# A streamed two-layer hybrid encoder: TensorE's order handed to the scheduler, more room ahead of side matmuls, memory held until DMAs have read it

## The chip, the cores and the metric

One core of one Trainium2 chip runs the whole program. The metric is the time of one execution on the device in microseconds (us). The kernel before was run three times. One further execution was taken by the hardware profiler; its trace gives the durations of instructions, waits and the granted TensorE clock.

## The reference

`x` is 256 positions by 2048 channels. Each of two layers normalises it, projects it into the columns of four token mixers and of four merge gates, mixes, projects each branch back to 2048 channels, merges by gates, and adds an output projection to the residual stream. All is float32.

```python
def hybrid_layer(x, ...):
    h = rms_norm(x, norm_g)
    proj = h @ w_in                       # (256, 2048) @ (2048, 15104)
...
    ya = a_bg * depthwise_conv(a_cg * a_x, conv_a_w) * silu(a_z)      # A: short convolution
    yb = gqa_attention(rope(rms(q)), rope(rms(k)), v) * silu(b_z)     # B: grouped-query attention
    yc = rwkv7_bidir(h, c_r, c_k, c_v, ...) * silu(c_z)               # C: RWKV-7, both directions
    u = depthwise_conv(d_val * sigmoid(d_gate), dw_w) + dw_b          # D: 31 taps, LayerNorm, swish
    yd = silu(layer_norm(u)) * silu(d_z)
...
    g = sigmoid(gates.reshape(b, s, 4, 2048) + b_gate)
    merged = sum(g * (ys @ w_branch))
    return x + merged @ w_out
def reference(x, ...):
    for l in range(2):
        x = hybrid_layer(x, ...)
    return rms_norm(x, final_norm_g)
```

## The kernel before, in words

**The main stream.** The weights of both layers lie in memory as 612 chunks of 128 x 1024 floats (512 KB), in the order of `STREAM` (line 90): three tiles of the RWKV decay weights (`L`), the input projections of branches C, B, A and D, the merges of branches A and B taken in turn, the D gates, the merge of D, the C gates (`c_z`), the merge of C, and the output projection (`O`). Each chunk is loaded by SP into `raw` (4 buffers). ScalarE (ACT) rounds it to `hi` (3 buffers), VectorE (DVE) makes `lo = raw - hi` (2 buffers), and TensorE (PE) multiplies: `tile_b` (459) takes two chunks for one tile of 128 columns, each with eight 128x512 matmuls of `hi` and eight 128x256 matmuls of `lo`, into a PSUM buffer `mg` (3 buffers). The activations lie as rounded pairs in `slab` tiles (`operand`, 486). `tile_branch` (469) does the same for the branch outputs into `mb` (1 buffer). Then ACT and DVE move the PSUM buffer into the arena (`whole`, 477).

**The side work.** All that the branches do between projection and merge is written as Python generators: `branch_a`, `branch_b`, `branch_d`, `rwkv`, and under it `inverses`, which inverts blocks of 64, and `chunks`, which prepares a stretch of the scan. Their matmuls go into PSUM buffers `sd` (4 buffers). The scan of one RWKV direction (lines 945 to 1027) is a chain: a product of `bdE` and `bdT`, moved by ACT to `j3`; products of `j3`, moved to `ls` and `hs`; a product of those and of the state `s0`, moved by ACT to `bdS`; a transpose of `bdS` through PE; and its move by ACT to the next `s0`. Sums over a head go through `parts` (616), which makes `part` (1 buffer, a rounded copy by ACT and a remainder by DVE), and two matmuls against `rounded`. `branch_d` (740) has two LayerNorm sums over 512 channels, each a matmul `sd<-arena,consts` of `sq`.

**What sets the order.** The program is traced once in Python. Every engine call passes `Engine.call` (line 202 of the profile is its `return f(out, ...)`, so that nearly all instructions have that line), which keeps a model of time: `now` for PE, `clk` for DVE and ACT, `due` for when the last result of the step is ready, and `landed` for DMAs. After every main matmul `pump` (343) lets each generator go on whose time `at` has come. `step` (330) runs it to its next `yield c` and sets `at`: `now + c` for c above 0, and for `yield 0` the time at which its results are due plus `SLACK` = 0.4. `drain` (348) lets nothing but side work go on until a generator has ended; a merge does so with its branch. PE then keeps the traced order, since `run` (1338) puts both layers under `manual_schedule` for PE. The orders of the other engines are made by the tile framework's scheduler.

**Memory.** The working tiles lie in one tile, `arena`, that the kernel hands out itself (`Arena`, 103): `a` (255) takes words, `f` (282) gives them back with a time `when`, the latest of `now`, `due` and `clk`, plus `OVER` = 1.5. `get` prefers words whose time has passed. The framework orders any two instructions that touch the same words. `room` (274) makes a generator wait until enough words are free. In branch D, `sq` can thus come to lie in words that a DMA of `rwkv` still reads (the `COPY` of 64x1024 into `xt`, and the two DMAs `scratch<-arena` of `xi` and `xt`, behind the 31 steps of the inverse on DVE).

**The layers' boundary.** `project` (1277) makes the new `x` in eight pairs of tiles. At the last one (g = 7) of layer 0 it sums the squares with three matmuls `sd<-arena,consts`, the last two of which read the squares of the last two tiles, and `new_rstd` makes the factor `rbc`. The next layer's first 8 tiles (`RAW`) are multiplied by the unnormalised `x` and scaled by `rbc` in `evac` (560), while `normalise` (541) makes `h`.

Of the kernel before, what the change touches and what calls it, by code (L numbers as in the profile page):

```python
# [18 lines left out]
P = 128  # L19
D = 2048  # L20
S = 256
# [81 lines left out]
class Arena:  # L103
# [11 lines left out]
    def get(self, words, keep=False, take=True, now=0.0):  # L115


        m = -(-words // self.U)
        best = None
        i = 0  # L120
        while i < self.n:
            if self.used[i]:
                i += 1
                continue
            e = i
            while e < self.n and not self.used[e]:
                e += 1
            if e - i >= m:

                j = i if keep else e - m  # L130
                late = self.when[j:j + m].max() > now
                key = (late, j) if keep else (late, e - i - m, -i)
                if best is None or key < best[0]:
                    best = (key, j)
            i = e
        if best is None:
            if not take:
                return False
            raise MemoryError(f"arena: {words} words asked, {(~self.used).sum() * self.U} free, live "
                              + str(sorted((v[1] * self.U, v[2]) for v in self.live.values())))  # L140
        j = best[1]
        if not take:
            return True
        self.used[j:j + m] = True
        self.peak = max(self.peak, int(self.used.sum()) * self.U * 4)
        return j, m
# [66 lines left out]
class Kern:  # L213
# [5 lines left out]
    SLACK = 0.4  # L219
    OVER = 1.5  # L220
    LEAD = 1.7
    TWAIT = 24.0
# [51 lines left out]
    def room(self, words):  # L274

        e = self.cur
        e.want, e.net = 0, 0
        while self.arena.free() < words + 640 + sum(max(0, x.want - x.net) for x in self.side):
            yield 0.4
        e.want = words  # L280

    def f(self, *aps):
        for ap in aps:
            _, m, _, j = self.arena.live.pop(id(ap))
            self.arena.put(j, m, max(self.now, self.due, *self.clk.values()) + self.OVER)
            if self.cur:
                self.cur.purse.net -= m * Arena.U
# [17 lines left out]
    def pside(self):  # L305
        self.ring = self.ring[1:] + [self.now + 1.5]
        return self.psum("sd", 4)


# [20 lines left out]
    def step(self, e):  # L330
        self.due = max(self.now, e.due)
        self.landed = 0.0
        self.cur = e
        c = next(e.gen, None)
        self.cur = None
        e.due = max(self.due, self.landed)
        if c is None:
            e.alive = False
            self.side.remove(e)
        else:  # L340
            e.at = self.now + c if c > 0 else e.due + self.SLACK

# [72 lines left out]
    def fetch(self):  # L415
        nc = self.nc
        while len(self.raws) < 1 + self.FAR and self.load():
            pass
        if not self.raws:
            return False  # L420
        raw = self.raws.pop(0)
        hi = self.wtile("hi", 3, F32R)
        lo = self.wtile("lo", 2, F32R)
        with self.tc.high_priority():
            nc.scalar.activation(hi, raw, AF.Copy)
            nc.vector.tensor_tensor(lo, raw, hi.bitcast(F32), ALU.subtract)
        self.ready.append((hi, lo))
        return True

    def chunk(self):  # L430
        while len(self.ready) < self.AHEAD and self.fetch():
            pass
        return self.ready.pop(0)

# [66 lines left out]
    def first_x(self):  # L501
        nc = self.nc
        self.l = 0
        self.xT = [self.operand() for _ in range(4)]
        self.xs = [self.a([P, 4, S], True) for _ in range(4)]
        with self.tc.high_priority(), self.tc.manual_schedule(engines={SP, ACT, DVE}):
# [32 lines left out]
            self.f(sq)  # L539

    def normalise(self, h):

        nc = self.nc
        for x in self.xs:
            n = x.shape[1]
            for j in range(0, n, 2):
                t = self.a([P, 2, S])
                for i in range(2):
                    nc.vector.scalar_tensor_tensor(t[:, i], x[:, j + i], self.pc("norm_g", self.hk + i), self.rbc,
                                                   ALU.mult, ALU.mult)  # L550
                yield 0
                o = h[self.hk // 4][:, self.hk % 4:self.hk % 4 + 2]
                self.split(o[:, :, 0, :], o[:, :, 1, :], t)
                self.f(t)
                self.hk += 2
                yield 0.4
            self.f(x)


    def evac(self, out, ps):  # L560
        self.whole(out, ps)
        if self.raw:
            self.nc.vector.tensor_tensor(out, out, self.rbc, ALU.mult)
# [69 lines left out]
    def head_rstd(self, x):  # L633

        nc = self.nc
        out = self.a1()
        nc.scalar.activation(out, x, AF.Square)
        parts = self.parts(out)
        yield 0
        ps = self.pside()[:, :S]  # L640
        self.rsqrt(ps, 1.0 / 64, self.e_rms, out, self.exact(ps, self.bdr, parts))
        yield 0
        return out

    def norm_rope(self, x, rs, g, dst):
        nc = self.nc
        xn = self.a1()
        nc.vector.scalar_tensor_tensor(xn, x, g, rs, ALU.mult, ALU.mult)
        t = self.a1()
        nc.vector.tensor_tensor(t, xn, self.cos, ALU.mult)  # L650
        parts = self.parts(xn)
        yield 0
        ps = self.pside()
        self.exact(ps[:, :S], self.permr, parts)
        nc.vector.tensor_tensor(xn, ps[:, :S], self.sin, ALU.mult)
        for sl, d in dst:
            nc.vector.tensor_tensor(d, t[sl], xn[sl], ALU.add)
        self.f(t, xn)
        yield 0

    def branch_b(self, k, v, qz):
# [12 lines left out]
        for i in range(NT):  # L674
# [12 lines left out]
            for tb in range(2):  # L687
# [16 lines left out]
                pes.append(pe)  # L704
                yield 0
            self.f(qr)
            for tb, pe in enumerate(pes):
                ps = self.pside()
                for h in range(2):
                    for kb in range(2):  # L710
# [4 lines left out]
                                     ps.rearrange("p (h k t) -> p h k t", h=2, k=2), AF.Copy)  # L715
                yield 0
            ps = self.pside()
# [22 lines left out]
    def branch_d(self, acc, convs, dz):  # L740
# [11 lines left out]
        nc.vector.tensor_tensor(sq[:, 0], sq[:, 0], sq[:, 1], ALU.add)  # L752
        yield 0
        ps = self.pside()
# [5 lines left out]
        nc.vector.tensor_tensor(sq[:, 0], sq[:, 0], sq[:, 1], ALU.add)  # L760
        yield 0
        ps = self.pside()
# [24 lines left out]
    def rwkv(self, rkv, tl, cz):  # L787
# [5 lines left out]
        for d in range(2):  # L793
# [8 lines left out]
            for p0 in range(0, NT, 2):  # L802
# [42 lines left out]
                parts = self.parts(rs)  # L845
                yield 0
                ps = self.pside()
# [41 lines left out]
                parts = self.parts(r2)  # L889
                yield 0  # L890
                ps = self.pside()
# [9 lines left out]
                for p in (p0, p0 + 1):  # L901
                    bd = self.bd["K"][0]
                    nc.scalar.activation(bd[lo, :, 0:CH], v4(al[lo, p]), AF.Copy)
                    nc.scalar.activation(bd[hi, :, CH:], v4(al[hi, p]), AF.Copy)
                    yield 0
                    ps = self.pside()
# [47 lines left out]
            for p in range(NT):  # L954
# [71 lines left out]
                parts = self.parts(sq)  # L1026
                yield 0
                ps = self.pside()
# [32 lines left out]
    def inverses(self, bd, gs, scr, ready):  # L1061
# [22 lines left out]
        for h in range(2):  # L1084
            nc.scalar.activation(w1[h * 64:h * 64 + 32], ps[h * 64:h * 64 + 32], AF.Copy)
        yield 0
        ps = self.pside().rearrange("p (c n) -> p c n", c=n)
# [5 lines left out]
        for h in range(2):  # L1093
            nc.scalar.activation(t[h * 64 + 32:h * 64 + 64, :, h * 64:h * 64 + 32], ps[h * 64:h * 64 + 32], AF.Copy)
        ready.extend(range(NT))
        yield 0

    def chunks(self, n, out, bd, al, vv, kb, gs, rd):
# [14 lines left out]
        nc.scalar.activation(rb[hi, :, CH:], rd[hi, p, cs2], AF.Copy)  # L1113
        yield 0
        ps = self.pside()
# [24 lines left out]
        out.append((ex, mk, w))  # L1140
        yield 0

# [108 lines left out]
    def merge(self, l, br, g, acc, mT, gens):  # L1251

        nc = self.nc
        first, last = br == BR_ORDER[0], br == BR_ORDER[-1]
        z = self.a([P, 2, S], True)
        for j in range(2):
# [20 lines left out]
    def project(self, l, mT):  # L1277
# [8 lines left out]
        for g in range(8):  # L1286
# [4 lines left out]
            if g < 7:  # L1291
# [5 lines left out]
                if g == 0:  # L1297
                    sq = s
                else:
                    nc.vector.tensor_tensor(sq, sq, s, ALU.add)  # L1300
                    self.f(s)
            else:

# [21 lines left out]
            for j in range(2):  # L1325
                k = 2 * g + j
                self.split(xT[-1][:, k % 4, 0, :], xT[-1][:, k % 4, 1, :], xr[:, j], self.pc("norm_g", k))
        self.new_rstd(sums)
        self.f(sq)
        self.xT, self.xs = xT, xs  # L1330
        if not last:
            return
        for g in range(8):
            e = nc.gpsimd if g in (3, 6) else nc.vector
            e.tensor_tensor(xs[g], xs[g], self.rbc[:, None, :].to_broadcast([P, 2, S]), ALU.mult)
            (nc.sync if g % 2 else nc.scalar).dma_start(io["out"][:, 2 * g:2 * g + 2], xs[g])

    def run(self):
# [4 lines left out]
        self.first_x()  # L1343

        with self.tc.manual_schedule(engines={mybir.EngineType.PE}):
            for l in range(DEPTH):
                self.layer(l)

# [124 lines left out]
```

## Time and profile before

| | |
|---|---|
| median of three runs | 2014.15 us (2011.96 to 2016.07) |
| the profiled execution | 2011.95 us, of which its span is 2009.7 us |
| mean granted TensorE clock | 0.990 of full speed |
| busy share of the span | PE 96%, DVE 72%, ACT 63%, POOL 4% |
| weights read | 612 DMAs of 512 KB; 332.48 MB read in all, 170 GB/s over the span |

In the trace a row gives engine, operation, what is written and read, its shape, and in brackets how long the engine was idle before it and what released it. `sd`, `mg` and `mb` are PSUM buffers, `arena` is any working tile.

### The profile page before, as it was taken

The numbers are of one execution on the slowest core, as the hardware profiler recorded it, in microseconds if no ns is written. First come the engines' busy times: TensorE is split into PE (matmuls) and PEld (weight loads), VectorE is DVE, ScalarE is ACT, GpSimd is POOL, SyncE is SP. The second block draws the span as 40 slices with busy tenths as digits, with TensorE's granted clock in tenths as the row PEclk, the third lists the DMA queues.
The fourth block names the chain that finished last, engine by engine and source line by source line (L and its number), as shares of the span: only waits on it lengthen the run. The fifth ranks groups of instructions, "written<-read, shape, count | busy, mean of one in ns | idle before, by whom it ended". The sixth has DMA issues, their size and how long they took to land.

```text
span 2009.7 us, 32327 instructions
## 1 busy us (share of the span) xinstructions
PE 1934.0 (96%) x12194; PEld 1707.4 (85%) x12194; DVE 1447.7 (72%) x2495; ACT 1261.3 (63%) x2293; POOL 71.3 (4%) x117
## 2 busy tenths in 40 slices
PE   8999999999989999999999999999999899999997
PEld 6887888888978998898888878889888789988886
DVE  7767969977786656666677778699767765566665
ACT  6676677676547765554556766776764577655544
POOL 1001010000110000000000011000001100000000
PEclk9999999999999999999999999999999899999998
DMA  7545444455654445656655545344555544456653
GB/s 248 177 159 157 158 150 142 147 175 174 188 167 137 147 151 186 210 192 216 207 181 178 163 156 166 127 147 159 175 172 189 160 137 153 159 193 204 204 193 128
DMA packets 97692, 343.17 MB, mean 171 GB/s; under 512 B 11808, under 2 KB 12192, under 8 KB 97536
## 3 DMA queue, kind: packets, MB, share of 16 engines
q1 hardware_dynamic: 93312, 331.48, 50.6%
q0 software_dynamic: 3648, 8.59, 1.7%
q8 instruction: 95, 1.56, 0.3%
q10 hardware_dynamic: 576, 1.05, 0.1%
q14 instruction: 61, 0.50, 0.1%
HBM read 332.48 MB, written 8.39 MB: 170 GB/s over the span
## 4 chain that ended last, share of the span: by engine, by line
PE 89%; DVE 6%; ACT 2%; DMA 1%; issue 1%; POOL 0%; DVEq 0%; SPq 0%; POOLq 0%; ACTq 0%
PE mg L202 71%; PE mb L202 9%; PE sd L202 9%; DVE arena L202 3%; DVE lo L202 2%; ACT arena L202 1%; ACT hi L202 1%; DVE slab L202 1%; DMA arena<-scratch 1%; DVE part L202 0%; DMA arena<-xT 0%; ACT L176 0%; DMA scratch<-arena 0%; ACT bdE L202 0%; ACT bdT L202 0%
## 5 line engine op out<-in xcount | busy, mean ns | idle before, releaser
L202 PE MATMUL mg<-slab,hi 128*128 128x512 f32 x4368 | 1148.8, 399 | 12.7 <-DVE slab L202 12.7
L202 DVE TENSOR_TENSOR lo<-raw,hi 128x1024 fp32r<-128x1024 f32 x612 | 748.0, 1222 | 368.6 <-PE mg L202 306.3
L202 PEld LDWEIGHTS mg<-slab,hi 128*128 128x128 f32 x4368 | 783.1, 190 | 152.2 <-DVE slab L202 15.3
L202 ACT ACTIVATE hi<-raw 128x1024 fp32r<-128x1024 f32 x612 | 646.3, 1057 | 413.3 <-PE mg L202 265.1
L202 PEld LDWEIGHTS mg<-slab,lo 128*128 128x128 f32 x4368 | 604.2, 191 | 46.1 <-issue 4.2
L202 PE MATMUL mg<-slab,lo 128*128 128x256 f32 x4368 | 634.1, 286 | 0.0
L202 DVE TENSOR_TENSOR arena<-arena 128x512 f32<-128x512 f32 (+15 forms) x389 | 165.8, 431 | 17.7 <-DMA scratch<-arena 6.4
L202 DVE SCALAR_TENSOR_TENSOR arena<-arena,par 128x256 f32<-128x256 f32 x346 | 154.5, 478 | 7.2 <-ACT arena L202 5.9
L202 PE MATMUL mb<-slab,hi 128*128 128x256 f32 (+1 forms) x1040 | 152.0, 286 | 0.0
L202 DVE TENSOR_TENSOR arena<-mg,arena 128x256 f32<-128x256 f32 x305 | 127.4, 418 | 16.3 <-ACT arena L202 10.8
L202 PEld LDWEIGHTS mb<-slab,hi 128*128 128x128 f32 x1040 | 136.1, 192 | 0.6
L202 ACT ACTIVATE arena<-arena 128x256 f32<-128x256 f32 (+4 forms) x195 | 94.0, 497 | 50.7 <-DVE arena L202 49.9
L202 ACT ACTIVATE arena<-arena,b_gate 128x256 f32<-128x256 f32 x128 | 64.5, 504 | 76.7 <-DVE arena L202 76.5
L202 ACT ACTIVATE arena<-mg 128x256 f32<-128x256 f32 x241 | 89.7, 372 | 18.3 <-PE mg L202 17.4
L176 ACT ACT_TABLE_LOAD x62 | 79.5, 1283 | 15.7 <-PE sd L202 13.8
L202 PE MATMUL mb<-slab,lo 128*128 128x256 f32 x528 | 87.5, 285 | 0.0
L202 DVE SCALAR_TENSOR_TENSOR arena<-arena,mb 128x512 f32<-128x512 f32 x64 | 43.8, 685 | 47.2 <-PE mb L202 45.8
L202 PEld LDWEIGHTS mb<-slab,lo 128*128 128x128 f32 x528 | 73.5, 191 | 0.2
L202 ACT ACTIVATE bdE<-sd 64x128 f32<-64x128 f32 x256 | 62.9, 269 | 8.4 <-PE sd L202 5.6
L202 ACT ACTIVATE arena<-sd 128x64 f32<-128x64 f32 (+4 forms) x122 | 40.6, 333 | 34.4 <-PE sd L202 32.4
L202 DVE SCALAR_TENSOR_TENSOR arena<-arena 128x256 f32<-128x256 f32 (+1 forms) x80 | 37.9, 474 | 15.0 <-ACT arena L202 12.4
L202 PE MATMUL sd<-part,rounded 128*128 128x512 f32 (+1 forms) x88 | 29.0, 378 | 20.0 <-DVE part L202 10.2
(96 smaller groups left out, 1052.4 us busy)
## 6 DMA issues: line engine op xcount, KB each, us to landing
raw<-w SPq DMA_DIRECT2D x612, 512.0 KB, 3.4
arena<-xT SPq DMA_DIRECT2D x4, 512.0 KB, 8.5
scratch<-slab POOLq DMA_DIRECT2D x16, 128.0 KB, 2.7
scratch<-arena POOLq DMA_DIRECT2D x8, 256.0 KB, 3.5
arena<-xT SPq DMA_DIRECT2D x8, 256.0 KB, 4.1
x<-arena SPq DMA_DIRECT2D x8, 256.0 KB, 3.7
arena<-x SPq DMA_DIRECT2D x8, 256.0 KB, 4.5
arena<-lorab POOLq DMA_DIRECT2D x16, 96.0 KB, 3.4
```

The source lines that it names most:

```text
L176: return f(out)
L202: return f(out, *args, **kw)
```

## The change

Six things are changed.

1. **PE's order.** `run` no longer puts the layers under `manual_schedule`; the scheduler orders PE as it does the other engines.
2. **Room ahead of matmuls.** In `step` a negative c now means `due - c`. Where the next step begins with a matmul, `yield 0` has become `yield self.MM` (1.0 us after the results are due; attention, head norms, branch D) or `yield self.MC` (0.7 us; RWKV), in place of 0.4. One more such yield stands at the end of `inverses`. The scan's own links keep `yield 0`.
3. **Memory and DMAs.** `f` counts freed words as used until at least `landed + 3.0`, so that words which a DMA reads are avoided for longer.
4. **Choice of words.** A long-lived tile (`keep`) takes the lowest free run that fits, whatever its time; the merge's `z` is no longer long-lived; `room` also asks for a contiguous run of up to `RUN` = 1056 words.
5. **`lo` later.** `fetch` makes only `hi`; `low` makes `lo` of a chunk when the chunk before it is taken up.
6. **The boundary.** At g = 7 of layer 0 the squares go into the same `sq` as those of the other pairs. One matmul sums them, in a generator `late_rstd` 2.5 us later. `evac` of an unnormalised tile and `normalise` wait for that generator.

```diff
-                late = self.when[j:j + m].max() > now
-                key = (late, j) if keep else (late, e - i - m, -i)
+                key = i if keep else (self.when[j:j + m].max() > now, e - i - m, -i)
...
+    MM = -1.0
+    RUN = 1056
+    MC = -0.7
...
-        while self.arena.free() < words + 640 + sum(max(0, x.want - x.net) for x in self.side):
+        while (self.arena.free() < words + 640 + sum(max(0, x.want - x.net) for x in self.side)
+               or not self.arena.get(min(words, self.RUN), take=False)):
             yield 0.4
...
-            self.arena.put(j, m, max(self.now, self.due, *self.clk.values()) + self.OVER)
+            self.arena.put(j, m, max(self.now, self.due, self.landed + 3.0, *self.clk.values()) + self.OVER)
...
-            e.at = self.now + c if c > 0 else e.due + self.SLACK
+            e.at = self.now + c if c > 0 else e.due - c if c < 0 else e.due + self.SLACK
...
-        lo = self.wtile("lo", 2, F32R)
         with self.tc.high_priority():
             nc.scalar.activation(hi, raw, AF.Copy)
-            nc.vector.tensor_tensor(lo, raw, hi.bitcast(F32), ALU.subtract)
-        self.ready.append((hi, lo))
+        self.ready.append([hi, None, raw])
+        if self.tiles == 0 and len(self.ready) < 3:
+            self.low(self.ready[-1])
         return True
+
+    def low(self, w):
+
+        if w[1] is None:
+            w[1] = self.wtile("lo", 2, F32R)
+            with self.tc.high_priority():
+                self.nc.vector.tensor_tensor(w[1], w[2], w[0].bitcast(F32), ALU.subtract)
 
     def chunk(self):
         while len(self.ready) < self.AHEAD and self.fetch():
             pass
-        return self.ready.pop(0)
+        w = self.ready.pop(0)
+        self.low(w)
+        if self.ready:
+            self.low(self.ready[0])
+        return w[:2]
...
+    def late_rstd(self, sq):
+
+        yield 2.5
+        sums = self.pside()[:, :S]
+        self.nc.tensor.matmul(sums, self.ones, sq[:, 0], start=True, stop=True)
+        self.new_rstd(sums)
+        self.f(sq)
+
     def normalise(self, h):
 
         nc = self.nc
+        while self.rstd and self.rstd.alive:
+            yield 0.3
...
         self.whole(out, ps)
+        if self.raw and self.rstd:
+            self.drain(self.rstd)
...
         parts = self.parts(out)
-        yield 0
+        yield self.MM
...
         nc.vector.tensor_tensor(sq[:, 0], sq[:, 0], sq[:, 1], ALU.add)
-        yield 0
+        yield self.MM
         ps = self.pside()
...
                 parts = self.parts(rs)
-                yield 0
+                yield self.MC
...
-        z = self.a([P, 2, S], True)
+        z = self.a([P, 2, S])
...
+            elif not last:
+                for j in range(2):
+                    ps = self.tile_b(mT)
+                    for i in range(2):
+                        nc.vector.tensor_tensor(xr[:, j], ps[:, i], xr[:, j], ALU.add)
+                nc.scalar.activation(s, xr, AF.Square)
+                nc.vector.tensor_tensor(sq, sq, s, ALU.add)
+                nc.vector.tensor_tensor(sq[:, 0], sq[:, 0], sq[:, 1], ALU.add)
+                self.tc.keep_in_program_order(nc.scalar.preload_act_table_set("natural_log"))
+                self.f(s)
+                self.rstd = self.add(self.late_rstd(sq), 99.0)
...
-
-        with self.tc.manual_schedule(engines={mybir.EngineType.PE}):
-            for l in range(DEPTH):
-                self.layer(l)
+        for l in range(DEPTH):
+            self.layer(l)
```

**DVE at branch D's first LayerNorm sum, layer 0.** Of the kernel before; the steps of the inverse are the adds on 64 partitions with shrinking widths, the `COPY` makes `xt`, the two `arena<-arena` adds on 128 partitions make `sq`, and the last row reads the sum's PSUM buffer.

```order
L202 TENSOR_TENSOR arena<-arena 64x3x29
L202 TENSOR_TENSOR arena<-arena 64x60
L202 TENSOR_TENSOR arena<-arena 64x2x30
L202 TENSOR_TENSOR arena<-arena 64x31 x2
L202 COPY arena<-arena 64x1024
L202 TENSOR_TENSOR arena<-arena 128x512
L202 TENSOR_TENSOR arena<-arena 128x256
L202 SCALAR_TENSOR_TENSOR arena<-sd_6010,arena 128x256 x4
L202 TENSOR_TENSOR lo_6001<-raw_5953,hi_6000 128x1024
```

Of the change, the same two adds and the reading row, in the midst of the inverse:

```order
L201 TENSOR_TENSOR arena<-arena 64x240
L201 TENSOR_TENSOR arena<-arena 128x512
L201 SCALAR_TENSOR_TENSOR arena<-arena,mb_5733 128x512
L201 TENSOR_TENSOR arena<-arena 64x20x12
L201 TENSOR_TENSOR arena<-arena 128x256
...
L201 TENSOR_TENSOR arena<-mg_5826,arena 128x256
L201 SCALAR_TENSOR_TENSOR arena<-sd_6005,arena 128x256 x4
L201 TENSOR_TENSOR arena<-arena 64x15x17
...
L201 TENSOR_TENSOR arena<-arena 64x2x30
L201 TENSOR_TENSOR arena<-arena 64x31 x2
L201 COPY arena<-arena 64x1024
```

The adds that make `sq`, and the row behind the sum, stood behind the `COPY`; now they stand 68 and 49 rows ahead of it.

**PE at the layers' boundary, after.** `mg_9962`, `mg_10019` and `mg_10075` are the first three tiles of layer 1, `slab_9834` holds the last four slices of the new `x`, and `sd_9985` is the sum of squares.

```order
L201 MATMUL mg_9962<-slab_9629,hi_9912 128x512 x4
L201 MATMUL mg_9962<-slab_9834,hi_9912 128x512 x2
L201 MATMUL mg_10019<-slab_9219,hi_9965 128x512
L201 MATMUL mg_9962<-slab_9834,hi_9912 128x512
L201 MATMUL mg_10019<-slab_9219,hi_9965 128x512 x3
L201 MATMUL mg_10019<-slab_9424,hi_9965 128x512 x4
...
L201 MATMUL mg_10019<-slab_9629,hi_9992 128x512 x4
L201 MATMUL mg_10019<-slab_9834,hi_9992 128x512 x3
L201 MATMUL sd_9985<-arena,consts 128x256
L201 MATMUL mg_10075<-slab_9219,hi_10022 128x512 x4
L201 MATMUL mg_10075<-slab_9424,hi_10022 128x512 x4
L201 MATMUL mg_9962<-slab_9834,hi_9912 128x512
```

The matmuls on `slab_9834` stand among those of the next tile, and the sum, one matmul where there were three, stands behind 46 main matmuls of layer 1; before, the last two sums stood ahead of the first matmul of layer 1.

**PE at the end of the second RWKV direction's scan, layer 1.** Of the kernel before:

```order
L202 MATMUL sd_17305<-arena,bdE_85 128x128
L202 MATMUL sd_17305<-arena 128x128
L202 MATMUL mg_17253<-slab_9971,lo_17228 128x256 x2
...
L202 MATMUL mb_17320<-slab_15732,hi_17256 128x256 x4
L202 MATMUL sd_17343<-consts,bdS_103 128x128
L202 MATMUL mb_17320<-slab_15732,hi_17256 128x256 x4
...
L202 MATMUL mg_17356<-slab_9970,hi_17291 128x512
L202 MATMUL sd_17368<-arena,bdE_85 128x64
L202 MATMUL sd_17368<-arena 128x64
L202 MATMUL mg_17356<-slab_9970,hi_17291 128x512 x3
...
L202 MATMUL mg_17356<-slab_9972,hi_17323 128x512 x4
L202 MATMUL sd_17401<-part_17378,rounded 128x512 x2
```

Of the change:

```order
L201 MATMUL sd_17458<-arena,bdE_85 128x128
L201 MATMUL sd_17463<-arena,bdM_89 128x128
L201 MATMUL sd_17463<-arena,bdM_89 128x64
L201 MATMUL sd_17458<-arena,bdE_85 128x64
L201 MATMUL sd_17487<-arena,bdE_85 128x128
L201 MATMUL sd_17487<-arena 128x128
L201 MATMUL sd_17513<-consts,bdS_103 128x128
L201 MATMUL sd_17539<-arena,bdE_85 128x64
L201 MATMUL sd_17539<-arena 128x64
L201 MATMUL sd_17574<-part_17549,rounded 128x512 x2
L201 MATMUL mg_17780<-slab_9958,hi_17731 128x512 x4
```

Between two links of the chain (`sd<-arena...`, then the transpose `sd<-consts,bdS`, then `sd<-arena...`, then the sums `sd<-part`) there stood matmuls of `mg` and `mb`; now ten rows of side work stand together, from the products of `sd_17458` to the first two sums, and the next `mg` matmul comes after them.

## Rows read from the trace of the kernel before

**Rows 1.** The page, busy time of each engine, its share of the span, instructions.
```profile
PE 1934.0 (96%) x12194; PEld 1707.4 (85%) x12194; DVE 1447.7 (72%) x2495; ACT 1261.3 (63%) x2293; POOL 71.3 (4%) x117
```

**Rows 2.** Windows: length; busy us of PE, PEld, DVE, ACT, POOL; clock; DMA; GB/s.
```profile
850.00:900.00 50.00, 50.00 (x319) 45.40 (x319) 29.46 (x35) 25.61 (x36) 0.00 (x0) 1.00 0.59 191
```

**Rows 3.** PE's waits over the span: total us, times, longest us.
```profile
PE sd L202 <- DVE arena L202: 18.8, 3, 9.7
PE mg L202 <- DVE slab L202: 12.7, 5, 9.6
PE sd L202 <- DVE part L202: 10.2, 17, 1.3
PE sd L202 <- ACT part L202: 9.7, 10, 1.7
PE sd L202 <- ACT bdT L202: 4.3, 4, 1.3
PE sd L202 <- ACT arena L202: 4.1, 4, 2.2
PE sd L202 <- ACT bdE L202: 2.3, 1, 2.3
PE sd L202 <- ACT bdS L202: 1.3, 4, 0.4
```

**Rows 4.** Timeline of PE, branch D's first sum in both layers: start, us, instruction.
```profile
576.67 2.00 PE L202 MATMUL mg<-slab,hi 128*128 128x512 f32 x8
578.51 1.12 PE L202 MATMUL mg<-slab,lo 128*128 128x256 f32 x8
...
600.22 1.22 PE L202 MATMUL sd<-arena,consts 128*128 128x256 f32 x2 [9.74 <-DVE arena L202]
...
602.10 1.91 PE L202 MATMUL mg<-slab,lo 128*128 128x256 f32 x8
603.80 3.02 PE L202 MATMUL mg<-slab,hi 128*128 128x512 f32 x8
...
1591.62 1.19 PE L202 MATMUL sd<-arena,consts 128*128 128x256 f32 x2 [8.49 <-DVE arena L202]
```

**Rows 5.** Timeline of DVE before the first of these sums.
```profile
594.14 1.03 DVE L202 COPY arena<-arena 64x1024 f32<-64x1024 f32 x1
599.02 1.15 DVE L202 TENSOR_TENSOR arena<-arena 128x512 f32<-128x512 f32 x2 [3.86 <-DMA scratch<-arena]
```

**Rows 6.** Timeline of PE at the layers' boundary.
```profile
1007.45 0.70 PE L202 MATMUL sd<-arena,consts 128*128 128x256 f32 x2 [2.18 <-ACT arena L202]
1007.80 3.12 PE L202 MATMUL mg<-slab,hi 128*128 128x512 f32 x8
```

**Rows 7.** Timeline, one wait for `part`: DVE and PE.
```profile
102.36 1.22 DVE L202 TENSOR_TENSOR lo<-raw,hi 128x1024 fp32r<-128x1024 f32 x1
...
104.63 0.68 DVE L202 TENSOR_TENSOR part<-arena,part 128x512 fp32r<-128x512 f32 x1
105.36 0.50 PE L202 MATMUL sd<-part,rounded 128*128 128x512 f32 x1 [1.01 <-DVE part L202]
```

**Rows 8.** Windows behind short waits, columns as in rows 2.
```profile
103.00:107.00 4.00, 2.33 (x12) 1.65 (x12) 3.89 (x11) 2.76 (x8) 0.00 (x0) 1.00 0.52 173
...
285.00:289.00 4.00, 4.00 (x21) 3.71 (x20) 0.10 (x1) 2.96 (x6) 0.00 (x0) 0.57 0.01 2
...
1277.00:1281.00 4.00, 3.03 (x13) 2.74 (x14) 0.00 (x0) 2.75 (x7) 0.00 (x0) 0.68 0.27 105
```

**Rows 9.** Groups of ACT by form: busy us, mean ns, idle before.
```profile
L202 ACT ACTIVATE bdS<-sd 64x64 f32<-64x64 f32 x96 | 20.9, 217 | 16.4 <-PE sd L202 15.3
...
L202 ACT ACTIVATE arena<-sd,arena 128x128 f32<-128x128 f32 x48 | 17.2, 359 | 7.3 <-PE sd L202 7.2
...
L202 ACT ACTIVATE part<-arena 128x512 fp32r<-128x512 f32 x24 | 14.9, 622 | 0.9 <-DVE arena L202 0.7
...
L202 ACT ACTIVATE arena<-sd 128x256 f32<-128x256 f32 x18 | 6.8, 380 | 8.6 <-PE sd L202 8.5
```

More of the change, by code (lines that the diff above doesn't have):

```diff
@@ L503, in first_x @@
         self.l = 0
+        self.rstd = None
         self.xT = [self.operand() for _ in range(4)]
@@ L658, in norm_rope @@
         self.f(t, xn)
-        yield 0
+        yield self.MM
     def branch_b(self, k, v, qz):
@@ L704, in branch_b @@
                 pes.append(pe)
-                yield 0
+                yield self.MM
             self.f(qr)
@@ L715, in branch_b @@
                                      ps.rearrange("p (h k t) -> p h k t", h=2, k=2), AF.Copy)
-                yield 0
+                yield self.MM
             ps = self.pside()
@@ L752, in branch_d @@
         nc.vector.tensor_tensor(sq[:, 0], sq[:, 0], sq[:, 1], ALU.add)
-        yield 0
+        yield self.MM
         ps = self.pside()
@@ L760, in branch_d @@
         nc.vector.tensor_tensor(sq[:, 0], sq[:, 0], sq[:, 1], ALU.add)
-        yield 0
+        yield self.MM
         ps = self.pside()
@@ L845, in rwkv @@
                 parts = self.parts(rs)
-                yield 0
+                yield self.MC
                 ps = self.pside()
@@ L889, in rwkv @@
                 parts = self.parts(r2)
-                yield 0
+                yield self.MC
                 ps = self.pside()
@@ L904, in rwkv @@
                     nc.scalar.activation(bd[hi, :, CH:], v4(al[hi, p]), AF.Copy)
-                    yield 0
+                    yield self.MC
                     ps = self.pside()
@@ L1026, in rwkv @@
                 parts = self.parts(sq)
-                yield 0
+                yield self.MC
                 ps = self.pside()
@@ L1085, in inverses @@
             nc.scalar.activation(w1[h * 64:h * 64 + 32], ps[h * 64:h * 64 + 32], AF.Copy)
-        yield 0
+        yield self.MC
         ps = self.pside().rearrange("p (c n) -> p c n", c=n)
@@ L1094, in inverses @@
             nc.scalar.activation(t[h * 64 + 32:h * 64 + 64, :, h * 64:h * 64 + 32], ps[h * 64:h * 64 + 32], AF.Copy)
+        yield self.MC
         ready.extend(range(NT))
@@ L1113, in chunks @@
         nc.scalar.activation(rb[hi, :, CH:], rd[hi, p, cs2], AF.Copy)
-        yield 0
+        yield self.MC
         ps = self.pside()
@@ L1140, in chunks @@
         out.append((ex, mk, w))
-        yield 0
+        yield self.MC
     def layer(self, l):
@@ L1327, in project @@
                 self.split(xT[-1][:, k % 4, 0, :], xT[-1][:, k % 4, 1, :], xr[:, j], self.pc("norm_g", k))
-        self.new_rstd(sums)
-        self.f(sq)
         self.xT, self.xs = xT, xs
@@ L1332, in project @@
             return
+        self.new_rstd(sums)
+        self.f(sq)
         for g in range(8):
```

## The prediction

> **What bounds the kernel now.** I read the page first. PE is busy for 1934.0 of 2009.7 us, DVE for 72% and ACT for 63% of them [rows 1], so PE is the bound and the question is where it stands still. In a stretch in mid-stream it doesn't: 50.00 of 50 us busy at a granted clock of 1.00 [rows 2]. PE's waits come next [rows 3]. They add up to 63.4 us; 9.6 of them are the first matmul's, before any weights are there. What the change can win is the other 53.8 us, what the clock loses behind the waits, and no more, because the main matmuls are the same in number and shape.
>
> Three kinds of wait stand out. Two waits of 9.74 and 8.49 us are branch D's first LayerNorm sum in the two layers [rows 4]. The timeline of DVE says why: the adds that make `sq` come 3.86 us after everything before them, and what released them was a DMA that still read the words [rows 5]. They also stand behind the `COPY` that ends the inverse, as the DVE rows with the change show. One wait of 2.18 us is the sum at the layers' boundary [rows 6]. The 27 waits for `part` make 19.9 us [rows 3]: a `lo` of 1.22 us and `part` itself, 0.68 us, lie between the request and PE's next matmul, which the written order forbids to step aside [rows 7].
>
> Then the clock. Behind the long wait eight matmuls of 128x512 take 3.02 us where they took 2.00, and eight of 128x256 take 1.91 where they took 1.12 [rows 4].
>
> **What the change removes.**
>
> (a) D's first sums. In the new order the adds stand 68 rows ahead of the `COPY`, in words that no DMA reads. Both waits go, 9.74 + 8.49 = 18.2, and twice the slow groups behind them, 2 x (1.02 + 0.79) = 3.6 [rows 4]: 21.8 us. Next to be late is the second sum, which stands some 28 us of main matmuls behind the first; the merge of D that needs it comes another 13 us or more later, so I cost it at nothing. If that cover failed, the merge would wait for D's chain, by up to what the first sum waited for, 9.7 us.
>
> (b) The boundary. One sum stands behind 46 matmuls of layer 1 and waits for nothing. The 2.18 us go, and so do 3.12 - 2.00 of slow clock [rows 6, 4]: 3.3 us. Between nothing and another 2.2 us could come back, if the tiles of layer 1 fill all `mg` buffers before `rbc` is made; I take nothing, since those matmuls last longer than the wait did.
>
> (c) `part`: 10.2 + 9.7 = 19.9 us [rows 3]. A matmul that is ready may now go first, and the planner asks for 1.0 or 0.7 us where it asked for 0.4.
>
> (d) The other side waits: `bdT` 4.3, `bdE` 2.3, `bdS` 1.3, from the three on `arena` of DVE 18.8 - 18.2 = 0.6, and half of the 1.9 us that ACT's `arena` has beside the boundary, since the last sum of the kernel stays: 9.4 us. With them go two stretches of low clock, 4 x (1 - 0.57) = 1.7 and 3.03 x (1 - 0.68) = 1.0 [rows 8]: 12.1 us.
>
> (e) `mg` on `slab`: 12.7 - 9.6 = 3.1 [rows 3], at the start and at merges. I take half, 1.6 us.
>
> That is 21.8 + 3.3 + 19.9 + 12.1 + 1.6 = 58.7. A scheduler orders by its own guess of durations, so I leave a tenth of (c) and (d) standing, 3.2 us: **55.5 us removed**. One matmul sum of the boundary's three is left; two of some 0.3 us are too little to count.
>
> **What it adds.** PE's order now mixes main and side work more loosely, and most links of a chain stand further apart than before. But in 28 places of the new order, less than 0.7 us of matmuls stands between a matmul and the PE result that it hangs on through ACT or DVE. They lie in five clusters at the end of RWKV scans; the PE rows with the change show one. There, the late scan still holds arena words that the gates' tiles are to be written to, so that PSUM buffers stay full, and no main matmul is ready to go between. No row shows these waits, so each is priced from the row of the operation that PE then waits for, and 0.1 us for its crossings:
>
> - 6 transposes behind `bdS`, two ACT rows of 217 ns [rows 9]: 6 x 0.55 = 3.3.
> - 6 products behind `s0`, 359 ns [rows 9], less 0.3 of matmuls between: 6 x 0.16 = 1.0.
> - 5 behind `j3`, 380 ns [rows 9], less little: 5 x 0.4 = 2.0.
> - 2 group norms, a square and a rounded copy of 622 ns each [rows 9], and 0.68 for the remainder [rows 7]: 2 x 2.1 = 4.3 with crossings.
> - 9 others at the mean wait for `part`, 19.9 / 27 = 0.74 [rows 3]: 6.7.
>
> 17.3 us in all. After each cluster the clock may fall; I take the mean of the two stretches above, 5 x 1.35 = 6.8. **Added: 24.1 us.**
>
> The bounds: nothing, if the engines run otherwise than the order's durations suggest and the clusters close up without a wait; and 28 x 1.7, the longest `part` wait [rows 3], with 5 x 1.8 of clock, 56.6. I take the middle value because the rows of the very operations give it.
>
> The clock deserves a second look. In 4 us with PE busy for only 2.33, the clock stayed at 1.00; in another 4 us with PE busy throughout, behind one wait of 1.3 for `bdT`, it fell to 0.57 [rows 8, 3]. So a short wait sometimes costs clock and mostly doesn't. The Trainium skill ("TensorE: Matmul & The Clock Gate", section "HAM oscillation — how this bites in real kernels") says that a kernel whose TensorE pauses again and again pays the restart at a low clock each time. By that rule the 28 places would pay 28 x 1.35 in place of 5 x 1.35; the rows agree for some waits and disagree for more.
>
> The late `lo` costs nothing as long as DVE has it ready one chunk ahead: 1.22 us [rows 7] against some 2.8 us that a chunk keeps PE busy [rows 4]. Where DVE is clogged, a chunk would wait up to 1.2 us. The choice of words, `RUN` and the extra `yield` move side work by less than a chunk, and PE's other work covers that.
>
> **The sum.** 2011.95 - 55.5 + 24.1 = 1980.6, so **1981 us**. The base is the profiled execution, which is 0.1% below the median of the runs, 2014.15.
>
> **The rivals.**
>
> *All gain.* The 28 places cost nothing, (a) to (e) go in full: 2011.95 - 58.7 = 1953 us. For it: PE has no wait in mid-stream [rows 2]. Against: at the clusters nothing else is left to run. Chance 0.12.
>
> *The `part` waits stay.* The single `part` buffer passes from use to use, and what delays it is DVE's queue [rows 7], which the change leaves as full as before. Then 0.9 x 19.9 = 17.9 of the gain is missing: 1981 + 17.9 = 1999 us. The Trainium skill ("Perfetto Trace Analysis", section "Optimization Strategy") says that one gap that keeps repeating can mean too little memory for the next tile; the 27 waits of one kind agree in form. Against: the chain to `part` is short, and with other matmuls to run PE needn't stand there. Chance 0.11.
>
> *Clock at every place.* Each of the 28 drops the clock: 23 x 1.35 = 31 us more, 2012 us, no change. For it the 0.57, against it the 1.00 [rows 8]. Chance 0.10.
>
> *Slower.* PE runs ahead on main work and then meets the RWKV scan late. The scan's words hold the gates' tiles in PSUM, and each of the 28 links costs what the longest link of the scan cost before, 2.3 us behind `bdE` [rows 3], since ACT and DVE have `hi`, `lo` and evacuations in front: 28 x 2.3 + 6.8 = 71.2 against 55.5, 2028 us. It decides from 1.9 us a link on: (55.5 + 4 - 6.8) / 28. For it: such a wait exists. Against: it is one of many; the four behind `bdS` have 1.3 us in all. Chance 0.15.
>
> That the change doesn't do what it says is excluded for D's sums and the boundary by the order; for `part` it is the second rival.
>
> **How the numbers follow.** The forecast has the remaining 0.52. Faster by over 0.2% (4 us, about what a measurement of this kernel can tell from no change): forecast, all gain and `part`, 0.75; within 0.2%: clock, 0.10; slower: 0.15. The forecast's own range is 1965 to 1999. The range of 8 in 10 leaves out the slower rival and some of the ends: 1953 to 2014, which takes in both bounds of the added waits.
>
> **What would show it.** In the changed profile, PE's waits should list no 9 us row on DVE's `arena`; the sum of waits on `part` should be below 3 us; no wait of 2 us at the boundary. PE's gaps should sit at the ends of scans, some 0.3 to 2 us each, 17 us in all, with the clock below 1.00 behind them. The prediction is wrong if the new waits are over 40 us or below 5, if `part` keeps 10 us or more, or if a wait of several us opens at a merge because PE has run ahead of its branch.

## The result and the profile after

The changed kernel takes 1988.5 us (median of four, 1986.08 to 1990.98) against 2013.97 us of the kernel before. The ratio is 0.9874, 95% interval 0.9856 to 0.9891: 25 us faster, where 31 were forecast (1981 us; range 1953 to 2014). The profiled execution took 1987.77 us, 24.2 less than that of before.

The page of the changed kernel, busy time of each engine, as in [rows 1]:

```profile
PE 1926.2 (97%) x12190; PEld 1710.6 (86%) x12190; DVE 1436.0 (72%) x2496; ACT 1265.2 (64%) x2292; POOL 71.3 (4%) x117
```

PE's waits, columns as in [rows 3]:

```profile
PE mg L201 <- DVE arena L201: 14.1, 4, 6.0
PE mg L201 <- DVE slab L201: 9.4, 1, 9.4
PE sd L201 <- ACT bdS L201: 6.3, 8, 2.2
PE sd L201 <- ACT part L201: 5.6, 3, 2.4
PE sd L201 <- ACT arena L201: 4.3, 11, 1.0
PE sd L201 <- DVE arena L201: 2.2, 3, 1.8
PE sd L201 <- DMA bdX<-scratch: 2.1, 1, 2.1
PE mb L201 <- DVE arena L201: 1.2, 2, 0.8
PE mg L201 <- DVE lo L201: 1.0, 3, 0.5
PE sd L201 <- DVE part L201: 0.2, 1, 0.2
```

They add up to 46.4 us, 47.0 with those too short for the list (span 1985.5 less busy 1926.2, less 12.3 behind the last matmul); before it was 63.4. The 32 waits behind `part`, `bdT` and `bdE` in [rows 3] are now four, and a new row leads: `mg` behind DVE's `arena`, four waits, 14.1 us. Branch D's first sums and the sum at the boundary, rows of PE's timeline, as in [rows 4] and [rows 6]:

```profile
571.54 0.60 PE L201 MATMUL sd<-arena,consts 128*128 128x256 f32 x2
...
997.15 0.59 PE L201 MATMUL sd<-arena,consts 128*128 128x256 f32 x2
...
1549.17 0.59 PE L201 MATMUL sd<-arena,consts 128*128 128x256 f32 x2
```

None has a bracket: PE doesn't wait there. Two of the new waits make up most of the 14.1. Here is the first, from the timeline of all engines:

```profile
770.06 0.43 PE L201 MATMUL sd<-arena 128*128 128x64 f32 x2 [0.29 <-ACT arena L201]
...
771.45 0.63 ACT L201 ACTIVATE part<-arena 128x512 fp32r<-128x512 f32 x1
...
772.13 0.50 PE L201 MATMUL sd<-part,rounded 128*128 128x512 f32 x1 [1.64 <-ACT part L201]
...
772.86 0.67 PE L201 MATMUL sd<-part,rounded 128*128 128x512 f32 x1 [0.22 <-DVE part L201]
773.55 1.28 ACT L175 ACT_TABLE_LOAD   x1 [1.47 <-PE sd L201]
774.85 0.69 ACT L201 ACTIVATE arena<-sd,eps 128x512 f32<-128x512 f32 x1
775.55 1.28 ACT L175 ACT_TABLE_LOAD   x1
776.84 0.63 ACT L201 ACTIVATE arena<-arena 128x512 f32<-128x512 f32 x1
777.50 0.69 DVE L201 TENSOR_TENSOR arena<-arena 128x512 f32<-128x512 f32 x1 [4.70 <-ACT arena L201]
778.23 0.38 ACT L201 ACTIVATE arena<-mg 128x256 f32<-128x256 f32 x1 [0.76 <-DVE arena L201]
...
779.03 0.42 DVE L201 TENSOR_TENSOR arena<-mg,arena 128x256 f32<-128x256 f32 x1
...
779.50 3.78 PE L201 MATMUL mg<-slab,hi 128*128 128x512 f32 x8 [5.98 <-DVE arena L201]
```

The `bdS` and `s0` links close up as the order showed. Then come the group norm's two sums, at 772.13 and 772.86. Behind them ACT works off the square root (two table loads of 1.28 us and two passes of 0.69 and 0.63), DVE multiplies at 777.50, and only then may ACT move the next `mg` buffer, at 778.23: that tile's words are those of the norm's `sq`. In the program the move at 778.23 writes 256 of the 512 words in which `sq` lay. PE, with no free `mg` buffer, starts again at 779.50. In layer 1 the same happens, again for 5.98 us, up to 1760.91.

Windows, columns as in [rows 2]: this wait, the work behind it, the second wait of 5.98 us, and the stretches behind waits of 2.20 us (for `bdS`, ended at 328.49), 2.37 us (for `part`, at 1463.20) and 2.05 us (for a DMA, at 1595.25):

```profile
772.00:779.00 7.00, 1.17 (x2) 0.37 (x2) 2.15 (x4) 4.34 (x6) 0.00 (x0) 0.57 0.05 22
779.00:784.00 5.00, 4.50 (x15) 3.72 (x16) 3.40 (x9) 2.69 (x6) 0.00 (x0) 0.57 0.00 0
...
1753.00:1760.00 7.00, 1.52 (x2) 0.57 (x2) 1.75 (x3) 4.60 (x6) 0.00 (x0) 0.50 0.00 0
...
328.00:332.00 4.00, 3.39 (x18) 3.20 (x19) 3.39 (x11) 2.10 (x8) 0.00 (x0) 0.66 0.00 0
...
1463.00:1467.00 4.00, 3.80 (x24) 3.42 (x25) 3.60 (x9) 3.31 (x10) 0.00 (x0) 1.00 0.37 132
...
1596.00:1600.00 4.00, 4.00 (x71) 3.37 (x70) 0.91 (x3) 1.95 (x5) 0.00 (x0) 0.62 0.48 187
```

The clock fell ahead of the waits of 5.98 us: the second of them began at 1754.93, and the whole window from 1753.00 stands at 0.50, the lower of the two levels (1.2 of 2.4 GHz). By the same levels 0.57 over the 7 us from 772.00 means that the clock fell at about 773.0, while the first wait began at 773.52. In both layers it fell in or just behind a wait of 1.64 us for the norm's `part`.

**The account of the profiled executions.** Waits: 63.4 to 47.0, -16.4 us. PE's busy time: 1934.0 to 1926.2, -7.8. Worked out from 4 us windows over the whole span, busy time times the missing share of the clock was 9.8 us before and is 8.9 now, so the clock gives 0.9 of the 7.8, an estimate from these windows.

### The profile page after: what moved, and what is told of

Same layout as the page of the kernel before. It is cut to its first block, busy times and chain, and to the rows that moved or that the text cites. A ratio compares the mean times of both kernels' runs of the same rounds, so it can differ in the third digit from the quotient of the medians.

```text
span 1985.5 us, 32442 instructions
## 1 busy us (share of the span) xinstructions
PE 1926.2 (97%) x12190; PEld 1710.6 (86%) x12190; DVE 1436.0 (72%) x2496; ACT 1265.2 (64%) x2292; POOL 71.3 (4%) x117
## 4 chain that ended last, share of the span: by engine, by line
PE 92%; DVE 2%; DMA 2%; ACT 2%; issue 1%; POOL 0%; DVEq 0%; SPq 0%; ACTq 0%; POOLq 0%
PE mg L201 74%; PE mb L201 9%; PE sd L201 9%; DVE arena L201 1%; DVE lo L201 1%; ACT arena L201 1%; DMA bdX<-scratch 1%; ACT hi L201 0%; DMA scratch<-arena 0%; DMA arena<-xT 0%; ACT L175 0%; DMA arena<-scratch 0%; DMA raw<-w 0%; POOL bdT L201 0%; ACT bdE L201 0%
## 5 line engine op out<-in xcount | busy, mean ns | idle before, releaser
L201 PE MATMUL mg<-slab,hi 128*128 128x512 f32 x4368 | 1113.6, 396 | 23.6 <-DVE arena L201 14.1
L201 PE MATMUL mg<-slab,lo 128*128 128x256 f32 x4368 | 615.3, 285 | 1.0 <-DVE lo L201 1.0
L201 PEld LDWEIGHTS mg<-slab,lo 128*128 128x128 f32 x4368 | 584.7, 191 | 35.1 <-issue 2.7
L201 DVE TENSOR_TENSOR arena<-arena 128x512 f32<-128x512 f32 (+17 forms) x390 | 166.0, 432 | 38.8 <-ACT arena L201 30.0
L201 DVE SCALAR_TENSOR_TENSOR slab<-arena,slab 128x512 fp32r<-128x512 f32 (+1 forms) x64 | 35.4, 554 | 25.8 <-ACT slab L201 25.5
L201 ACT ACTIVATE arena<-arena,par 128x256 f32<-128x256 f32 x88 | 42.2, 509 | 6.2 <-DVE arena L201 4.8
```

The lines of the kernel that those rows point to most:

```text
L201: return f(out, *args, **kw)
```

## The experiments

Theory 1: the waits that are left come from PE's free order, which runs main work ahead of the RWKV chain until the chain's memory holds up the PSUM buffers. Theory 2: the free order is what took the old waits away, and the planner's parts only come along.

**e1: PE's order by hand again, all else changed.**

```diff
-        for l in range(DEPTH):
-            self.layer(l)
+        with self.tc.manual_schedule(engines={mybir.EngineType.PE}):
+            for l in range(DEPTH):
+                self.layer(l)
```

> The changed kernel, with PE's traced order restored; the other five parts stay. Theory 1 (PE's free order is what brings the new waits: it runs ahead, and at the ends of scans the PSUM buffers are full): the two 6 us waits of mg, the two group-norm chains of 1.9 us and most of the 6.3 us behind bdS go, with some 8 us of clock; the D sums stay cured by the planner's memory, the part waits by its room: about 1988 - 25 = 1963 us. Theory 2 (PE's free order is what removed the waits): the 19.9 us of part and most of the other side waits come back, 2005 to 2012 us.

1973.81 us, 0.9803 [0.9783, 0.9823]: 15 us faster than the change itself. PE's waits:

```profile
PE mg L201 <- DVE slab L201: 11.5, 5, 8.4
PE sd L201 <- DVE arena L201: 8.6, 5, 2.4
PE sd L201 <- DVE part L201: 6.7, 10, 1.7
PE sd L201 <- ACT arena L201: 3.4, 2, 2.4
PE sd L201 <- ACT bdE L201: 2.9, 2, 1.5
PE sd L201 <- ACT part L201: 1.3, 3, 0.5
```

The 14.1 us row and `bdS` are gone. `part` keeps 8.0 us of its 19.9, D's first sums wait for 2.38 and 2.40 in place of 9.74 and 8.49, and the boundary still waits, 2.44. So neither theory has it all: the planner's parts by themselves take most of the old waits away, and the free order, put on top, takes most of the rest and adds more than that.

**e2: PE's order free, all else as before.**

```diff
-        with self.tc.manual_schedule(engines={mybir.EngineType.PE}):
-            for l in range(DEPTH):
-                self.layer(l)
+        for l in range(DEPTH):
+            self.layer(l)
```

> The kernel before, with nothing changed but PE's order, left to the scheduler. Theory 1: part waits mostly go (PE has other matmuls), D's sums no longer hold PE up for 9 us since PE goes past them, but waits at the ends of scans come, about as many as in the changed kernel: 1985 to 2000 us, and the planner's parts are worth little on top only because the free order eats them. Theory 2: this part alone carries the gain, 1988 us or below.

1985.72 us, 0.9866 [0.9847, 0.9885]: the change's own time, from one of its six parts. Both theories had this number, and it doesn't separate them; the waits tell more:

```profile
PE mg L202 <- DVE arena L202: 14.3, 3, 6.5
...
PE sd L202 <- ACT bdS L202: 6.3, 5, 2.0
```

`part` is down to 3.5 us in all, and the two waits of `mg` behind the scans are there, 6.07 and 6.52. D's sums and the boundary cost PE nothing although the old code makes them, and although DVE still waits for the scratch DMA ahead of `sq`; this is DVE's timeline:

```profile
599.66 1.15 DVE L202 TENSOR_TENSOR arena<-arena 128x512 f32<-128x512 f32 x2 [1.58 <-DMA scratch<-arena]
```

PE has other work meanwhile.

**e3: only the time of freed memory.**

```diff
-            self.arena.put(j, m, max(self.now, self.due, *self.clk.values()) + self.OVER)
+            self.arena.put(j, m, max(self.now, self.due, self.landed + 3.0, *self.clk.values()) + self.OVER)
```

> The kernel before, with nothing changed but freed memory counted as used until 3.0 us after the last DMA of the step has landed. If memory under the DMAs makes D's first sum wait: that wait goes in layer 0, where the sum's rows now stand ahead of the COPY, and not in layer 1, where they still stand behind it: 2014 - 11 = 2003 us. If it's the order of PE that makes it: 2014 us, both waits there.

2010.24 us, 0.9984 [0.9974, 0.9995]; the profiled execution was the slowest of the ten, 2014.31. PE at D's sums in layer 0 and at the first in layer 1:

```profile
595.31 0.59 PE L202 MATMUL sd<-arena,consts 128*128 128x256 f32 x2
...
605.21 1.22 PE L202 MATMUL sd<-arena,consts 128*128 128x256 f32 x2 [3.72 <-DVE arena L202]
...
1594.77 1.19 PE L202 MATMUL sd<-arena,consts 128*128 128x256 f32 x2 [8.50 <-DVE arena L202]
```

As the memory theory says, the first sum of layer 0 is cured and that of layer 1 is not. But a part of it comes back at once: the second sum, which had been hidden, now waits for 3.72 behind the inverse's steps on DVE. The gain is some 4 us, not 11.

**e4: the late scan's memory held.** In the changed kernel, for the last pair of the second direction:

```diff
-                self.f(sq)
+                if d == 1 and p == 3:
+                    held.append(sq)
+                else:
+                    self.f(sq)
...
-        self.f(ysum)
+        self.f(ysum, *held)
```

and the same for `y2`, and for `hs` and `ls`.

> The changed kernel, with the memory of the second direction's last scan stretch and group norm (sq, y2, hs, ls) not given back before the branch's end, so that the gates' tiles can't be put into it. Theory 1: the two waits of 5.98 us, in which the move out of mg waits for the words of sq, go or shrink to under 2 us, and with them the low clock behind: 1988 - 12 to 16 = 1972 to 1976 us. Rival (PE simply has nothing else to do at that point, because the merge of C needs the chain's result, or the memory merely comes from another late tile): 1986 to 1989 us, with the waits in place.

1968.88 us, 0.9782 [0.9759, 0.9804]: 20 us faster than the change, where 12 to 16 were expected. The place that stood still for 5.98 us, in PE's timeline:

```profile
767.12 0.33 PE L201 MATMUL sd<-consts,bdS 128*128 128x128 f32 x1 [0.54 <-ACT bdS L201]
...
769.27 3.30 PE L201 MATMUL mg<-slab,hi 128*128 128x512 f32 x8 [0.93 <-DVE arena L201]
```

The wait is 0.93, and `mg` now goes ahead of the norm's sums. In layer 1 no `mg` matmul waits for `arena` there any more, and the two waits of 1.64 us for the group norms' `part` went too. Only the time at which four tiles are given back was changed, so it is shown that these tiles' memory made the waits.

**e5 and e6: two of the planner's parts undone, with PE's order by hand.** e5 is e1 with

```diff
-    MM = -1.0
+    MM = -0.4
-    MC = -0.7
+    MC = -0.4
```

> As e1 (the changed kernel with PE's traced order), with 0.4 us of room ahead of steps that begin with a matmul, as before the change. If that room is what spares the waits for part where PE's order is fixed: of 19.9 us of part waits before and 8.0 in e1, most come back, 12 us, and D's sums with them by some 2: 1974 + 14 = 1988 us. If the part waits depend on the planner's other parts (memory, late lo): 1972 to 1978 us.

2003.43 us, 0.9947 [0.9926, 0.9968], 30 us above e1, where 14 were expected.

```profile
PE sd L201 <- DVE arena L201: 17.0, 6, 8.8
...
PE sd L201 <- ACT part L201: 10.5, 11, 1.7
PE sd L201 <- DVE part L201: 5.7, 11, 1.0
PE sd L201 <- DMA bdX<-scratch: 4.6, 1, 4.6
```

`part` is back at 16.2 us, D's first sum in layer 1 at 8.79, and a wait of 4.6 for a DMA is new. The adds that make `sq` wait for the scratch DMA again, although the landed term is in; this is DVE's timeline:

```profile
1582.96 1.15 DVE L201 TENSOR_TENSOR arena<-arena 128x512 f32<-128x512 f32 x2 [2.52 <-DMA scratch<-arena]
```

e6 is e1 without the landed term:

```diff
-            self.arena.put(j, m, max(self.now, self.due, self.landed + 3.0, *self.clk.values()) + self.OVER)
+            self.arena.put(j, m, max(self.now, self.due, *self.clk.values()) + self.OVER)
```

> As e1, without counting freed memory as used until the DMAs have landed. If that term is what cures D's first sums: their waits go from 2.4 back to 8 to 10 us in one layer or both, with 2 us of clock each: 1974 + 8 to 18 = 1982 to 1992 us. If the other rules of memory (the choice of words, the contiguous run) or the shift of the steps do it: 1972 to 1977 us, with both waits near 2.4.

1974.77 us, 0.9806 [0.9784, 0.9827]: e1's time, with the sums waiting for 2.38 and 2.51. My leading guess fell: counting memory under DMAs isn't what cures D's sums here. Of the planner's parts, the room ahead of matmuls is worth 30 us where PE's order is fixed, and this term nothing measurable. The choice of words, the late `lo` and the boundary were not undone one by one.

**e7: the kernel before, PE's order free, memory held as in e4.** (The edits of e2 and e4.)

> As e2 (the kernel before, PE's order left to the scheduler), with the memory of the second direction's last scan stretch held to the branch's end, as in e4. If the free order and the held memory do nearly all, and the planner's other parts add little under a free order: the two waits of 6.1 and 6.5 us and their clock go, 1986 - 12 to 19 = 1967 to 1974 us, about e4's time. If the planner's parts carry a share of their own (boundary, D, kz): 1978 us or more.

1961.43 us, 0.9743 [0.972, 0.9766]: faster than both kernels and than every other run here, and below the 1967 to 1974 expected.

```profile
PE mg L202 <- DVE slab L202: 9.0, 2, 8.7
PE sd L202 <- ACT bdS L202: 6.9, 6, 2.0
...
PE mg L202 <- DVE lo L202: 3.1, 4, 1.4
```

The `mg` row behind `arena` is empty. The other five parts of the change are not needed for this.

**e8: times made longer.** e4 with

```diff
-                key = i if keep else (self.when[j:j + m].max() > now, e - i - m, -i)
+                key = (self.when[j:j + m].max() > now, j if keep else e - i - m, -i)
...
-    OVER = 1.5
+    OVER = 4.0
```

> As e4, with the planner's allowance for freed memory raised from 1.5 to 4.0 us, and long-lived tiles again avoiding words whose time hasn't passed. If late memory makes the remaining waits at the scans too (bdS 4.7, arena of ACT 2.9 beside the last sum, mg on arena 4.0): about half of the 11.6 us goes, 1969 - 6 = 1963 us. If those links wait because the scheduler put them close together whatever the memory: 1967 to 1972 us.

1976.12 us, 0.9809 [0.9783, 0.9834]: slower than e4, and neither of the numbers expected.

```profile
PE mg L201 <- DVE arena L201: 19.9, 3, 7.9
PE mg L201 <- DVE slab L201: 9.3, 1, 9.3
```

There are fewer waits, but three of `mg` behind `arena`, 5.3, 6.7 and 7.9 us, at other places (271, 480 and 1454 us). The two rules together move the collision to other tiles; they don't end it. Which of the two does it wasn't tested.

**e9, e10 and e11.** e9 is the changed kernel with the room of e5.

> The changed kernel, PE's order free, with 0.4 us of room ahead of steps that begin with a matmul, as before the change. With PE's order by hand that room was worth 30 us (e1 against e5). If a free order does the same work itself, the room is worth nothing here: 1985 to 1992 us, part waits still under 8 us. If it adds to the free order: 1995 us or more.

1989.1 us, 0.987 [0.9855, 0.9885]: in the changed kernel with its free order the room is worth nothing, as expected. The waits are others, though: `mg` behind `arena` has seven, 12.7 us, the longest 4.0. e10 is e4 with `sq` alone held.

> The changed kernel, with only the last group norm's sq held to the branch's end, y2, hs and ls given back as before. If the two waits of 5.98 us come from the words of sq alone: they go as in e4, 1969 to 1973 us. If any memory of the late chain does it, the gates' tiles are put into y2, hs or ls instead: one wait of 3 to 7 us stays in at least one layer, 1975 to 1988 us.

1980.87 us, 0.9826 [0.9808, 0.9845]. PE's timeline in layer 0 and in layer 1:

```profile
773.16 2.12 PE L201 MATMUL mg<-slab,hi 128*128 128x512 f32 x8 [0.93 <-DVE arena L201]
...
1760.71 1.65 PE L201 MATMUL mg<-slab,hi 128*128 128x512 f32 x3 [6.52 <-DVE arena L201]
```

In layer 0 the wait shrank as in e4, in layer 1 it is 6.52: `sq` isn't the only tile of the late chain that does it. In the program of e10 the `mg` move that ends this wait writes 256 words of `y2`, and it stands behind the last operation that reads them. e11 is e4 with the room of e5.

> As e4 (the changed kernel with the late scan's memory held), with 0.4 us of room. e4 took 1969 us and e7, the kernel before with a free order and the same memory held, 1961 us. If the room is what costs e4 those 7 us (steps come later, and chains with them): 1960 to 1964 us. If the choice of words or the boundary does: 1967 to 1972 us.

1975.23 us, 0.9804 [0.9786, 0.9821]: slower than e4 by some 5 us, so that with the memory held the room is worth something even in a free order. The room isn't what separates e4 from e7, and the two numbers expected both missed. What does is open. In the traces PE waits for 33.6 us in e4 and 27.2 in e7; e4 alone has a wait of 2.56 for `part`, one of 2.91 for a DMA and 4.0 of `mg` behind `arena`.

## Why the prediction was right, and where it was off

**What was removed** came nearly as forecast: 50.6 us of waits where the terms have 48.1. (a) D's two waits are gone. (b) The boundary's is gone, but not through the single late sum: e2 has the old sums and no wait, e1 the new one and 2.44 us. (c) Of 19.9 us of `part`, 5.8 are left, and 3.5 of these are the group norms that I had counted as added; 2.4 remain where I had left 2.0. So the sign "on `part` below 3 us" failed, and it didn't fit the forecast's own 4.3 for the group norms. (d) `bdT` and `bdE` are gone from the list. (e) `mg` on `slab` has only the first matmul's wait, so 3.1 went, not 1.6.

**What was added** was priced too low by half. I had 17.3 us. Without the first matmul (9.4), the last sum (1.0) and the old kind of `part` (2.4), the trace has 47.0 - 12.8 = 34.2. Term by term: `bdS` 6.3 against 3.3 (four of the eight waits are 0.54, as priced, but two are 1.17 and 2.20); `s0` and `j3`, 3.3 against 3.0; group norms 3.5 against 4.3. The step that failed is "9 others at the mean wait for `part`, 19.9 / 27 = 0.74: 6.7". They measured some 20 us: the `mg` and `mb` rows behind `arena` (14.1 and 1.2), `sd` on DVE's `arena` 2.2, a DMA 2.1, `lo` 1.0. Two of them were the first main matmul behind a cluster, at 5.98 us each, where the forecast had gaps of 0.3 to 2 us. I had priced the chain up to the norm's sums, and not on to what the next `mg` buffer hangs on, though the prediction itself names the late scan's words as what fills the buffers. The rows to price it by were there, in the same trace: a square root is two table loads and two passes.

**The clock** came out right in its sum: -0.9 us measured, -0.6 by the forecast's terms (7.4 of slow clock removed, 6.8 added). That is luck, since both terms were some 2 us too small. All the slow stretches of before went, 9.8 us, and four others came, 8.9 us: at three clusters, not five, and behind the DMA wait at 1595.25. Term (a) shows why: for each of D's waits it took the clock of two groups of matmuls, 1.8 us, while in the windows of that trace from 600 to 608 us busy time times the missing clock is 2.9. Behind the 5.98 us waits the clock stood at 0.57 and, in layer 1, at 0.50 for 5 us. Behind a wait of 2.37 us it stayed at 1.00, while behind waits of 2.20 and 2.05 us it stood at 0.66 and 0.62 (the last three windows). This is the wait of 2.37, in PE's timeline:

```profile
1463.20 0.50 PE L201 MATMUL sd<-part,rounded 128*128 128x512 f32 x1 [2.37 <-ACT part L201]
```

The Trainium skill ("TensorE: Matmul & The Clock Gate", section "HAM oscillation — how this bites in real kernels") describes a kernel that waits for a DMA in every pass of its loop and restarts at a low clock each time. Here the work behind the waits of 5.98, 2.20 and 2.05 us ran at a low clock, and the work behind this one didn't, so the 28 restarts that the prediction reckons by that rule didn't come.

**What makes up for half the error** wasn't in the forecast: of the 7.8 us that PE's busy time fell by, 6.9 aren't the clock's. That the forecast came within 6 us is luck to this extent. The account: 14.4 too much expected of the waits (-30.8 against -16.4), 0.3 too little of the clock, 6.9 not foreseen; 31.4 - 24.2 = 7.2. Where the 6.9 come from isn't shown. A part can be estimated: a 128x512 matmul behind a wait keeps PE busy for 0.50 us [rows 7], one of eight in a row for 2.00 / 8 = 0.25 [rows 4], and PE's listed waits went from 48 to 37, which gives 11 x 0.25 = 2.8. e1, with PE's order by hand, has a busy time of 1921.8 and 3.2 of slow clock by the same windows, 5.6 less than before in the same sense, so it isn't the free order alone.

**The rivals.** "All gain" fell with the new waits. "The `part` waits stay" fell for the change, and for both of its ways: with a free order they are 3.5 us (e2), with room and a fixed order 8.0 (e1). The Trainium skill's remark that one repeating gap can mean too little memory for the next tile ("Perfetto Trace Analysis", section "Optimization Strategy") didn't hold for `part`, which still has its single buffer. The new `mg` waits are for memory, but not for want of it: they go when tiles lie elsewhere (e4). "Clock at every place" fell. "Slower" had its mechanism right, the scan's memory holding up PSUM, and its price wrong: 34.2 us over some 28 places is 1.2 a link, short of the 1.9 from which it would have decided.

## What to carry to other kernels

A fixed order with room and a free order are two cures for the same waits: the free order alone was worth 28 us (e2), the planner's parts with a fixed order 40 (e1), and together they gave 25. A free order with the late tiles held gave 55 (e7). Before you free the bound engine's order, see what its buffers are emptied into; if a planner hands out that memory by its own idea of time, the scheduler will keep the dependencies but not the times, and a tile of a late chain can stop the main stream. Price a cluster of side work up to the next main matmul, not up to its own last one.

## What the runs showed of the hardware

Two ACT table loads of 1.28 us each stand in the group norm's chain, 2.56 of the 5.98 us wait; in the kernel before, PE had no wait behind that chain. And the length of a wait alone didn't tell what the clock did: waits of 2.37 and 1.80 us left the granted clock at 1.00 (windows from 1463 and 1209 us), while 0.66 and 0.62 stood behind waits of 2.20 and 2.05.
